# The head of a pooling and state-space layer: x scaled before it is transposed, dt taken from unsplit h, and another written order

## Chip, cores, metric

The kernel runs on one core of a Trainium2 chip. The metric is the time of one execution in microseconds (us) as the device measures it; lower is better. Times are medians of several runs on the same chip.

A core has five engines with an instruction stream each: TensorE (PE in the profile, its weight loads PEld), VectorE (DVE), ScalarE (ACT), GpSimd (POOL) and SyncE (SP), which here only issues DMA transfers. ACT issues some DMAs too. Results of matmuls go to PSUM, everything else on the chip to SBUF.

## The reference, cut to what matters

One layer of inference on a prompt of 1024 rows and 64 sample rows (8 sequences of 8), 1088 rows of 1024 channels together, all in fp32:

```
shift, scale, gate = split(silu(c) @ w_ada + b_ada, 3)
h = rmsnorm(x, norm_g) * (1 + scale) + shift
u_pool, z_pool, z_ssm, xbc, dt_raw, g_raw = split(h @ w_in)
p  = (pool_mix(u_pool) * silu(z_pool)) @ w_pool_out
dt = softplus(dt_raw + dt_bias)
y  = ssd(silu(conv(xbc)), dt, ...) ; y = rmsnorm(y * silu(z_ssm), ssm_norm_g)
s  = y @ w_ssm_out
x  = x + gate * ((sigmoid(g_pool) * p + sigmoid(g_ssm) * s) @ w_o)
out = rmsnorm(x, final_g)
```

Outputs are the normalised rows and the new states of the pooling, the convolution and the recurrence.

## The kernel before, in words

Matmuls of full precision are made from reduced-precision ones: an operand is split into a high part (`whi`, `hh_`) made by ACT and a low part (`wlo`, `hl_`), the rest, made by DVE or POOL; a product is then three matmuls, high by high, high by low and low by high. h is kept transposed, channels on partitions: eight tiles `tf[k]` of 128 channels by 1088 rows in fp32, and `hh_[k]`, `hl_[k]`.

The change lies in `first()`, the head, and in what it calls. There the order on all five engines is the written one: `in_line` chains the instructions of each engine as they are written. Behind it a scheduler orders by priority, and may put instructions of later units between those of `first()`.

The head runs through these stages:

1. **Turning x.** Nine row tiles (eight of 128 rows, one of 64) are loaded. For each, the sum of squares is taken by DVE or ACT (`x_square`), then a root by ACT (`x_root`) and a reciprocal by DVE (`x_unit`), in groups of rows 0 and 1, 2 to 4, 5 to 8. `x_unit` also builds for each row tile the diagonal matrix of the reciprocals, and `x_turn` multiplies x by it on PE (L228), which transposes and scales at once. `x_copy` takes the result from PSUM to `tf`, by DVE and ACT in turn. A step is one group and one k; `x_turns(2, ...)` is the third group, block 2 of the columns. PSUM comes in 5 buffers `ps` (`PB()`) and 3 buffers `mm` (`PA()`).
2. **Coefficients.** `ada_mm`, `ada_out`, `ada_end` compute scale and shift (`md`) in three parts, for k 0 and 1, 2 and 3, and 4 to 7. `ada_end` transposes the result (L286).
3. **h.** `h_make(block, ks)` applies scale and shift: ACT writes the high part, DVE or ACT the fp32 value in place in `tf`, DVE the low part (L309).
4. **First products.** `products(block, ks)` makes two tiles of the sigmoid gate from h and weights directly (L883 to L885). `done` applies the sigmoid and stores. `gate_load` and `gate_mm` (L839) make the residual gate in eight steps on the side; four loads wait until an earlier step frees a buffer.
5. **dt.** `dt_block` multiplies h by 32 columns of `w_in` (L733), in four column groups of PE. It reads high and low part one after the other, both as fp32.
6. **Sums.** `combine()` makes the sums of blocks of h that a Strassen-Winograd scheme with seven products needs (S1, S2, S3, and S4, which replaces parts of `hh_` and `hl_`), in the place of `tf`, and splits them: high halves by ACT (L481, L504), low halves by DVE (L482, L497). It is a generator; each `next(sums)` issues a piece.
7. **First pair.** `strassen(..., early=True)` runs the seven products of a pair of output tiles; a product is 24 matmuls with 272 columns (L603 to L605). Its weights w[0] to w[6] are prepared by `first_steps` (differences L549, splits L160 and L163, low parts by DVE), stepped by `next(wst)`. `hook(n)`, called behind product n, issues the sums and weight splits that later products need. Products 3 (the fourth), 4, 5 and 6 read S2, S3, S1 and S4.

After the head come the other pairs, in the same scheme with POOL making the low parts, then the pooling and state-space work.

Of the kernel before, what the change touches and what calls it, by code (L numbers as in the profile page):

```python
# [8 lines left out]
F32 = mybir.dt.float32  # L9
F32R = mybir.dt.float32r  # L10
AF = mybir.ActivationFunctionType
ALU = mybir.AluOpType
# [8 lines left out]
P = 128  # L21
# [20 lines left out]
HF, SB = T // 2, T // 4  # L42
# [4 lines left out]
def tile_pool_ssd_step(  # L47
# [9 lines left out]
    def nm(s):  # L57
        uid[0] += 1
        return f"{s}_{uid[0]}"
# [30 lines left out]
    def R(shape=(P, T), dt=F32):  # L90
        return hs.tile(list(shape), dt, tag="R", name=nm("R"), bufs=3)
# [7 lines left out]
    def PA():  # L99
        return psA.tile([P, 512], F32, tag="mm", name=nm("mm"))  # L100
# [108 lines left out]
    def x_unit(a, b):  # L209
        n = xr[a][1]  # L210
        V.reciprocal(rs[:n, a:b], rs[:n, a:b])
        if not dg:
            dg.append(R())
        for i in range(a, b):
            n = xr[i][1]
            V.tensor_scalar(dg[0][:n, i * P:i * P + n], ident[:n, :n], rs[:n, i:i + 1], None, ALU.mult)

    tf = [None] * KT

    def x_turn(g3, k):  # L220

        if g3 == 0:
            tf[k] = tfp.tile([P, T], F32, tag="tf", name=nm("tf"), bufs=8)
        px = PB()
        c = 0
        for i in range((0, *XG)[g3], XG[g3]):
            xt, n = xr[i]
            mm(px[:, c:c + n], xt[:n, k * P:(k + 1) * P], dg[0][:n, i * P:i * P + n], start=True, stop=True)  # L228
            c += n
        return g3, k, px, c  # L230

# [243 lines left out]
    def combine():  # L475
        L_, R_ = slice(0, HF), slice(HF, T)

        big = []

        def parts(src, hi, lo):  # L480
            act(hi, src, AF.Copy)  # L481
            V.tensor_tensor(lo, src, hi.bitcast(F32), ALU.subtract)  # L482

        def room(lst, k):
            if lst is S1:
                lst[k] = (hs.tile([P, 2, HF], F32R, tag="sq", name="S1", bufs=1) if k == 3 else R((P, 2, HF), F32R))
            else:
                if k == 0:
                    big.append(Y4(hs).rearrange("p k (j n) -> p k j n", j=2))
                lst[k] = big[-1][:, k]  # L490

        def part(lst, k, src):
            room(lst, k)
            parts(src, lst[k][:, 0], lst[k][:, 1])

        def low(k):
            V.tensor_tensor(S2[k][:, 1], tf[k][:, L_], S2[k][:, 0].bitcast(F32), ALU.subtract)  # L497
        for k in range(4):
            a, b = tf[k], tf[k + 4]
            room(S2, k)  # L500
            V.tensor_tensor(b[:, R_], a[:, R_], b[:, R_], ALU.add)
            V.tensor_tensor(a[:, R_], a[:, L_], a[:, R_], ALU.subtract)
            V.tensor_tensor(a[:, L_], b[:, R_], a[:, L_], ALU.subtract)
            act(S2[k][:, 0], a[:, L_], AF.Copy)  # L504
            if k:
                low(k - 1)
            if k < 3:
                yield
        low(3)
        yield  # L510
        for k in range(4):
            part(S3, k, tf[k][:, R_])
        yield
        for k in range(4):
            a, b = tf[k], tf[k + 4]
            V.tensor_tensor(b[:, L_], b[:, L_], a[:, L_], ALU.subtract)
            part(S1, k, b[:, R_])
            if k % 2:
                yield
        for k in range(4):  # L520
            parts(tf[k + 4][:, L_], hh_[k][:, R_], hl_[k][:, R_])
            if k % 2:
                yield

# [196 lines left out]
    def dt_w():  # L721
        raw = tfp.tile([P, KT, NH], F32, tag="dtw", name="dtw", bufs=1)
        load(raw, w_in[0, :, C_DT:C_DT + NH].rearrange("(k p) c -> p k c", p=P))
        return raw

    def dt_block(w, i):
        o, n = BLK[i]
        ps = PA()
        for kk in range(2):
            for part in (hh_, hl_):  # L730
                for r in range(4):
                    k = 4 * kk + r
                    mm(ps[32 * r:32 * r + 32, :n], w[:, k, :], part[k][:, o:o + n].bitcast(F32),  # L733
                       start=(kk == 0 and part is hh_), stop=(kk == 1 and part is hl_))
        s = pa.tile([P, HF], F32, tag=("s1", "u2", "u3")[i], name=nm("dts"))
        act(s[:, :n], ps[:, :n], AF.Identity, bias=dtb[:, 0:1])
        store_(dts_d[:, o:o + n], s[:, :n])

# [115 lines left out]
    def first():  # L854
# [14 lines left out]

        banks = {}  # L870

        def products(bi, ks):
            o, n = BLK[bi]
            for t in range(2):
                if (bi, t) not in banks:
                    banks[bi, t] = (PB if (bi, t) in ((1, 1), (2, 0), (2, 1)) else PA)()[:, :n]
            for k in ks:
                for t in range(2):
# [4 lines left out]
                    mm(ps, a, rh, start=(k == 0), stop=False)  # L883
# [3 lines left out]
        tags = iter(("s1", "u2", "u3", "c2", "s1", "u2"))  # L887

        def done(bi, t):
            o, n = BLK[bi]  # L890
# [66 lines left out]
        for k in range(4, 8):  # L957
            ada_load(2, k)
        next(late)
        mr = ada_out(1)  # L960
        products(2, range(1))
        ada_end(1, mr)
# [11 lines left out]
        for k in range(4, KT):  # L974
            ada_mm(2, k)
        mr = ada_out(2)
        products(2, range(3, 4))
        dtw = dt_w()
        run, (wz, wst) = light[0][1], light[0][0]()
        bg = gate_bias()  # L980
        for k in range(4):
            gate_load(k)
        next(wst)
        ada_end(2, mr)

        for bi in range(3):
            h_make(bi, range(4, 8))
        for bi in range(3):
            products(bi, range(4, 8))
            for k in range(2 * bi, min(2 * bi + 2, 4)):  # L990
                gate_mm(k)
                gate_load(k + 4)

        sums = combine()
        next(late)
        for bi in range(3):
            done(bi, 0)
            done(bi, 1)
            next(sums)
        dt_block(dtw, 0)  # L1000
        dt_block(dtw, 1)
        next(sums)
        next(wst)
        dt_block(dtw, 2)
        next(sums)
        for k in range(4, 8):
            gate_mm(k)
        gate_end(bg)
        next(late, None)

        def hook(n):
            if n in (0, 2):
                next(wst)
            if n < 2:
                next(sums)
            if n in (3, 4):
                next(wst)
                next(sums)
        run(wz, hook)
        in_line(every)  # L1020
# [915 lines left out]
```

## Time and profile before

| | |
|---|---|
| Median of 3 runs | 1301.33 us (1299.25 to 1301.85) |
| Profiled execution: its own time | 1298.25 us |
| Profiled execution: span | 1296.5 us, 26406 instructions |
| PE busy | 1261.6 us |
| DVE, ACT, POOL busy | 887.8, 696.2, 675.4 us |
| Granted clock of PE, mean | 0.996 |
| HBM | 167.06 MB read, 83.01 MB written |

In the time-order rows a line gives start, length, engine, line of the kernel, operation, result and operands, shapes and count, and in brackets the idle time of the engine just before and what ended it. Rows of groups give busy us and mean ns of one, then idle time. An fp32 matmul leaves two records, a transpose one. Ends of matmuls are modelled, since they are pipelined; starts are the better measure on PE.

### The profile page before, as it was taken

To read this page: it belongs to the slowest core of one execution; us is meant where nothing else is said; L and a number is where in the kernel's file an instruction comes from. 1 tells how busy PE (TensorE), PEld (TensorE's weight loads), DVE (VectorE), ACT (ScalarE), POOL (GpSimd) and SP (SyncE) were. 2 spreads that over 40 slices of the span, in tenths; PEclk is the share of its full clock that TensorE was granted. 3 is DMA by queue.
4 is the path that set the end of the run, shared out by engine and by line. 5 is a ranking of instruction groups with operands and counts; after the bars stand their busy time and mean duration, and the time that the engine had idled before them with its cause. 6 is when DMAs were issued, how large, how long until landed. Compare 5 with 4: busy or idle time off the path is not lost. (4 is left out here: it accounts for less than half of the span.)

```text
span 1296.5 us, 26406 instructions
## 1 busy us (share of the span) xinstructions
PE 1261.6 (97%) x9739; PEld 1168.5 (90%) x9739; DVE 887.8 (68%) x1512; ACT 696.2 (54%) x1656; POOL 675.4 (52%) x563
## 2 busy tenths in 40 slices
PE   7999999999999999999999999999999999999998
PEld 6779999989999999998889999888888888999786
DVE  4685778866978678775767665477565878476433
ACT  5664356375656564545455464676887766201111
POOL 1007668677869776664344453366676656214000
PEclk9999999999999999999999999999999999999999
DMA  9837345465455544444556455999988665475631
GB/s 331 255 110 232 109 157 174 136 212 162 153 183 198 157 159 129 159 135 128 160 154 194 148 170 174 346 358 364 312 282 277 203 204 163 170 268 160 228 105 50
DMA packets 233793, 251.68 MB, mean 194 GB/s; under 512 B 31265, under 2 KB 177905, under 8 KB 233658
## 3 DMA queue, kind: packets, MB, share of 16 engines
q1 hardware_dynamic: 161568, 171.60, 41.7%
q10 hardware_dynamic: 72098, 78.41, 17.6%
q8 instruction: 77, 1.26, 0.4%
q14 instruction: 50, 0.41, 0.1%
HBM read 167.06 MB, written 83.01 MB: 193 GB/s over the span
## 5 line engine op out<-in xcount | busy, mean ns | idle before, releaser
L163 POOL TENSOR_TENSOR wlo<-rawA,whi 128x512 fp32r<-128x512 f32 x120 | 185.3, 1549 | 188.1 <-ACT whi L160 101.7
L163 POOL TENSOR_TENSOR wlo<-raw,whi 128x512 fp32r<-128x512 f32 x92 | 151.1, 1650 | 121.9 <-ACT whi L160 112.8
L354 PE MATMUL mm<-Y,whi 128*128 128x352 f32 (+1 forms) x480 | 163.3, 340 | 0.9 <-DVE G L1785 0.7
L355 PE MATMUL mm<-Y,whi 128*128 128x352 f32 (+1 forms) x480 | 157.4, 328 | 1.0 <-DVE Y L1459 1.0
L356 PE MATMUL mm<-Y,wlo 128*128 128x352 f32 (+1 forms) x480 | 156.8, 327 | 0.0
L605 PE MATMUL mm<-Y,wlo 128*128 128x272 f32 x496 | 143.6, 290 | 4.5 <-POOL wlo L163 4.1
L603 PE MATMUL mm<-Y,whi 128*128 128x272 f32 x496 | 146.4, 295 | 0.2
L603 PE MATMUL ps<-Y,whi 128*128 128x272 f32 x496 | 144.4, 291 | 1.4 <-ACT o L803 1.4
L604 PE MATMUL ps<-Y,whi 128*128 128x272 f32 x496 | 143.1, 289 | 0.0
L604 PE MATMUL mm<-Y,whi 128*128 128x272 f32 x496 | 142.9, 288 | 0.0
L605 PE MATMUL ps<-Y,wlo 128*128 128x272 f32 x496 | 142.6, 288 | 0.0
L160 ACT ACTIVATE whi<-rawA 128x512 fp32r<-128x512 f32 x125 | 78.1, 626 | 97.0 <-PE ps L604 43.2
L1051 DVE SCALAR_TENSOR_TENSOR GA<-GA,cvT,GA 128x1112 f32<-128x1112 f32 x72 | 126.7, 1763 | 0.6 <-ACT GA L1048 0.5
L160 ACT ACTIVATE whi<-raw 128x512 fp32r<-128x512 f32 x96 | 58.7, 626 | 91.2 <-DVE raw L549 43.0
L605 PEld LDWEIGHTS mm<-Y,wlo 128*128 128x128 f32 x496 | 93.4, 188 | 6.4 <-POOL wlo L163 5.4
L354 PEld LDWEIGHTS mm<-Y,whi 128*128 128x128 f32 x480 | 90.2, 188 | 6.9 <-issue 4.3
L603 PEld LDWEIGHTS ps<-Y,whi 128*128 128x128 f32 x496 | 93.3, 188 | 2.7 <-ACT o L803 1.6
L603 PEld LDWEIGHTS mm<-Y,whi 128*128 128x128 f32 x496 | 93.3, 188 | 2.3 <-issue 0.8
L604 PEld LDWEIGHTS mm<-Y,whi 128*128 128x128 f32 x496 | 93.4, 188 | 0.7 <-issue 0.6
L604 PEld LDWEIGHTS ps<-Y,whi 128*128 128x128 f32 x496 | 93.3, 188 | 0.3 <-issue 0.2
L605 PEld LDWEIGHTS ps<-Y,wlo 128*128 128x128 f32 x496 | 93.4, 188 | 0.2 <-issue 0.2
L1196 ACT ACTIVATE dec<-dec,acT 128x128 f32<-128x128 f32 (+1 forms) x288 | 86.7, 383 | 10.0 <-POOL dec L1187 6.3
(445 smaller groups left out, 3790.3 us busy)
## 6 DMA issues: line engine op xcount, KB each, us to landing
rawA<-in_w_in SPq DMA_DIRECT2D x46, 512.0 KB
dec<-acs_d SPq DMA_DIRECT2D x32, 512.0 KB
xbc<-GA ACTq DMA_DIRECT2D x24, 512.0 KB
xb<-xbc SPq DMA_DIRECT2D x32, 384.0 KB
rawA<-in_w_in SPq DMA_DIRECT2D x32, 256.0 KB
pw<-in_w_ssm_out ACTq DMA_DIRECT2D x32, 256.0 KB
ws<-ph ACTq DMA_DIRECT2D x32, 256.0 KB
ws<-pw SPq DMA_DIRECT2D x32, 256.0 KB
```

The source lines that it names most:

```text
L160: ins = act(hi[:, :, :ncols], raw[:, :, :ncols], AF.Copy)
L163: (eng or nc.gpsimd).tensor_tensor(lo[:, :, :ncols], raw[:, :, :ncols], hi[:, :, :ncols].bitcast(F32), ALU.subtract)
L354: mm(ps[:, :n], a, rh[k][:, o:o + n], start=(k == 0), stop=False)
L355: mm(ps[:, :n], a, rl[k][:, o:o + n], start=False, stop=False)
L356: mm(ps[:, :n], b, rh[k][:, o:o + n], start=False, stop=(k == nk - 1))
L603: mm(p, hi, ah, start=(k == 0), stop=False)
L604: mm(p, hi, al, start=False, stop=False)
L605: mm(p, lo, ah, start=False, stop=(k == 3))
L1051: V.scalar_tensor_tensor(d[:, :n], rp[:, k:k + n], cvT[:, 24 * k + mc:24 * k + mc + 1], d[:, :n], ALU.mult, ALU.add)
L1196: act(dec[:, h], dec[:, h], AF.Exp, bias=acT[:S, c, 8 * g + h:8 * g + h + 1], scale=-1.0)
```

## The change

- Rows 0 and 1 of x are turned as before. Rows 2 to 8 are scaled in place by their reciprocals (3, 6 and 8 by ACT, the others by DVE), and turned by a transpose against the identity.
- `dt_block` reads h from `tf` before the sums overwrite it, with half the matmuls; its bias, copy and store become `dt_out`. Blocks 0 and 1 come behind `products(1, ...)`, block 2 in front of the last product step of block 2. Then come the sums.
- The sums come in another order: the second and third weight step are put in front of and behind S2; S3 behind product 0, S1 in one piece behind product 2 without the last subtraction; this stands directly in front of each S4 split, behind products 3 and 4.
- The products of block 2 with k = 3 are halved around the third `ada_end`; h and products of blocks 0, 1, 2 alternate; the sigmoids of block 0 come before the h of block 2.
- `dt_w` and some buffer tags are moved.

```diff
         if not dg:
-            dg.append(R())
+            dg.append(R((P, 2 * P)))
         for i in range(a, b):
-            n = xr[i][1]
-            V.tensor_scalar(dg[0][:n, i * P:i * P + n], ident[:n, :n], rs[:n, i:i + 1], None, ALU.mult)
+            xt, n = xr[i]
+            if i < 2:
+                V.tensor_scalar(dg[0][:n, i * P:i * P + n], ident[:n, :n], rs[:n, i:i + 1], None, ALU.mult)
+            elif i in (3, 6, 8):
+                act(xt[:n], xt[:n], AF.Copy, scale=rs[:n, i:i + 1])
+            else:
+                V.tensor_scalar(xt[:n], xt[:n], rs[:n, i:i + 1], None, ALU.mult)
...
-            mm(px[:, c:c + n], xt[:n, k * P:(k + 1) * P], dg[0][:n, i * P:i * P + n], start=True, stop=True)
+            if i < 2:
+                mm(px[:, c:c + n], xt[:n, k * P:(k + 1) * P], dg[0][:n, i * P:i * P + n], start=True, stop=True)
+            else:
+                nc.tensor.transpose(px[:, c:c + n], xt[:n, k * P:(k + 1) * P], ident[:n, :n])
...
         for k in range(4):
+            part(S1, k, tf[k + 4][:, R_])
+        yield
+        for k in range(4):
             a, b = tf[k], tf[k + 4]
             V.tensor_tensor(b[:, L_], b[:, L_], a[:, L_], ALU.subtract)
-            part(S1, k, b[:, R_])
-            if k % 2:
-                yield
-        for k in range(4):
-            parts(tf[k + 4][:, L_], hh_[k][:, R_], hl_[k][:, R_])
+            parts(b[:, L_], hh_[k][:, R_], hl_[k][:, R_])
             if k % 2:
                 yield
...
-        ps = PA()
+        ps = (PA if i < 2 else PB)()
         for kk in range(2):
-            for part in (hh_, hl_):
-                for r in range(4):
-                    k = 4 * kk + r
-                    mm(ps[32 * r:32 * r + 32, :n], w[:, k, :], part[k][:, o:o + n].bitcast(F32),
-                       start=(kk == 0 and part is hh_), stop=(kk == 1 and part is hl_))
-        s = pa.tile([P, HF], F32, tag=("s1", "u2", "u3")[i], name=nm("dts"))
+            for r in range(4):
+                k = 4 * kk + r
+                mm(ps[32 * r:32 * r + 32, :n], w[:, k, :], tf[k][:, o:o + n], start=(kk == 0), stop=(kk == 1))
+        return ps
+
+    def dt_out(i, ps):
+        o, n = BLK[i]
+        s = pa.tile([P, HF], F32, tag=("u3", "c2", "s1")[i], name=nm("dts"))
         act(s[:, :n], ps[:, :n], AF.Identity, bias=dtb[:, 0:1])
         store_(dts_d[:, o:o + n], s[:, :n])
...
         mr = ada_out(2)
-        products(2, range(3, 4))
-        dtw = dt_w()
+        products(2, range(3, 4), (0,))
...
+        ada_end(2, mr)
+        products(2, range(3, 4), (1,))
+        h_make(0, range(4, 8))
+        products(0, range(4, 8))
+        gate_mm(0)
+        gate_load(4)
+        h_make(1, range(4, 8))
         next(wst)
-        ada_end(2, mr)
-        for bi in range(3):
-            h_make(bi, range(4, 8))
-        for bi in range(3):
-            products(bi, range(4, 8))
-            for k in range(2 * bi, min(2 * bi + 2, 4)):
-                gate_mm(k)
-                gate_load(k + 4)
+        products(1, range(4, 8))
+        done(0, 0)
+        done(0, 1)
+        dts = [dt_block(dtw, i) for i in range(2)]
+        h_make(2, range(4, 8))
+        products(2, range(4, 7))
+        dts.append(dt_block(dtw, 2))
+        for i in range(3):
+            dt_out(i, dts[i])
+        products(2, range(7, 8))
+        for k in range(1, 4):
+            gate_mm(k)
+            gate_load(k + 4)
+        next(late)
+        next(wst)
         sums = combine()
-        next(late)
-        for bi in range(3):
-            done(bi, 0)
-            done(bi, 1)
-            next(sums)
-        dt_block(dtw, 0)
-        dt_block(dtw, 1)
+        next(sums)
+        done(1, 0)
+        done(1, 1)
+        next(sums)
+        next(sums)
+        done(2, 0)
+        done(2, 1)
         next(sums)
         next(wst)
-        dt_block(dtw, 2)
-        next(sums)
         for k in range(4, 8):
             gate_mm(k)
         gate_end(bg)
         next(late, None)
         def hook(n):
-            if n in (0, 2):
+            if n in (1, 3, 4):
                 next(wst)
-            if n < 2:
-                next(sums)
-            if n in (3, 4):
-                next(wst)
+            if n in (0, 2, 3, 4):
                 next(sums)
```

More of the change, by code (lines that the diff above doesn't have):

```diff
@@ L870, in first, with products @@
         banks = {}
-        def products(bi, ks):
+        def products(bi, ks, ts=range(2)):
             o, n = BLK[bi]
@@ L877, in products @@
             for k in ks:
-                for t in range(2):
+                for t in ts:
                     ps = banks[bi, t]
@@ L885, in products @@
                     mm(ps, a, rl, start=False, stop=(k == KT - 1))
-        tags = iter(("s1", "u2", "u3", "c2", "s1", "u2"))
+        tags = iter(("s1", "u2", "u2", "u3", "c2", "s1"))
         def done(bi, t):
@@ L959, in first @@
         next(late)
+        dtw = dt_w()
         mr = ada_out(1)
```

## Prediction

> **What bounds the kernel now.** I read the page first, then the chain of waits of TensorE, then the head of the kernel in time order, engine by engine, since every edit lies in the first 105 us.
>
> ```profile
> span 1296.5 us, 26406 instructions
> PE 1261.6 (97%) x9739; PEld 1168.5 (90%) x9739; DVE 887.8 (68%) x1512; ACT 696.2 (54%) x1656; POOL 675.4 (52%) x563
> ```
>
> TensorE (PE) is busy 97% of the span and idle 35 us in all. Whoever wants time must take work from PE, or the place where PE waits; and work taken from PE counts only where PE is what ends last. So I cut the head into stretches (columns: length, then busy us of PE, PEld, VectorE = DVE, ScalarE = ACT, GpSimd = POOL with instruction counts, granted clock, DMA share, GB/s).
>
> ```profile
> 9.70:10.70 1.00, 1.00 (x4) 1.00 (x5) 1.00 (x2) 0.46 (x2) 0.00 (x0) 1.00 1.07 418
> 11.70:12.70 1.00, 1.00 (x7) 1.00 (x6) 0.04 (x1) 0.90 (x2) 0.00 (x0) 1.00 0.99 397
> 13.70:14.70 1.00, 1.00 (x11) 1.00 (x11) 0.91 (x5) 0.41 (x2) 0.00 (x0) 1.00 0.88 165
> 66.40:79.30 12.90, 12.90 (x147) 7.17 (x146) 11.42 (x18) 8.04 (x16) 0.00 (x0) 1.00 0.52 190
> 79.30:100.00 20.70, 20.12 (x157) 19.67 (x157) 19.04 (x34) 13.71 (x26) 1.76 (x1) 1.00 0.24 75
> ```
>
> Two things show. From 66.4 to 100 us DVE is busy 30.5 of 33.6 us: it is nearly as full as PE, with the sums of h. And PE's first matmuls run slowly: 4, then 7, then 11 records in a microsecond of the same work, although the granted clock says 1.00 throughout.
>
> **Turning x.** Now the rows that price the first edit.
>
> ```profile
> 20.39 0.94 PE L228 MATMUL ps<-R,Y 128*128 128x128 f32 x6
> 21.25 0.43 PE L228 MATMUL ps<-R,R 64*128 64x64 f32 x2
> 21.61 0.94 PE L228 MATMUL ps<-R,Y 128*128 128x128 f32 x6
> ...
> 29.77 0.33 PE L286 MATMUL ps<-ident,mr 128*128 128x128 f32 x1
> ...
> 50.91 0.47 PE L883 MATMUL ps<-Y,whi 128*128 128x448 f32 x1
> 52.23 0.38 PE L286 MATMUL ps<-ident,mr 128*128 128x128 f32 x2
> ...
> 834.38 0.60 PE L1400 MATMUL ps<-ident,xb 128*128 128x128 f32 x4
> 834.81 0.27 PE L1402 MATMUL ps<-ident,xb 128*128 128x128 f32 x1
> ```
>
> Each matmul of x by a diagonal leaves two records. A step of the third group (rows 5 to 8) takes 21.61 - 20.39 = 1.22 us, three full rows of it 0.86. A transpose against the identity leaves one record, and four take 834.81 - 834.38 = 0.43, so 0.11 each: a third-group step becomes 0.44, a second-group step (rows 2 to 4) 0.32 instead of 0.86. On PE that removes 8 x 0.78 + 8 x 0.54 = 10.6 us. The other end is the cadence of L228's records, 0.86 / 6 = 0.14, which would leave 1.0 to 1.5 us of it behind; I take 0.11, from the same instruction.
>
> The price is on the other engines: seven rows of 1024 must be scaled before they can be turned.
>
> ```profile
> 13.97 0.68 DVE L216 TENSOR_SCALAR R<-ident,rs 128x128 f32<-128x128 f32 x3
> 17.43 1.22 DVE L201 SCALAR_TENSOR_TENSOR sqj<-Y 128x1024 f32<-128x1024 f32 x1
> ...
> 19.42 0.29 ACT L207 ACTIVATE rs<-ss,eps 128x4 f32<-128x4 f32 x1
> 19.74 0.18 DVE L211 RECIPROCAL rs<-rs 128x4 f32<-128x4 f32 x1 [0.62 <-ACT rs L207]
> ...
> L1896 DVE TENSOR_SCALAR q<-q,sso 128x640 f32<-128x640 f32 x1 | 0.6, 553 | 0.1
> L203 ACT ACTIVATE sqj<-Y 128x1024 f32<-128x1024 f32 x3 | 3.1, 1046 | 0.0
> ```
>
> A diagonal costs DVE 0.68 / 3 = 0.23; a row scaled by DVE lies between the 0.55 of 640 elements and the 1.22 of the two-read operation on 1024. Between 0.23 at 128 and 0.55 at 640 lies 0.63 ns an element, so 1024 take an estimated 0.79. ACT takes 1.05 for 1024. At the second group DVE scales two rows instead of building three diagonals (+0.9), which moves its last square from 17.43 to about 18.3 and its end to 19.5: about when the root of the last four stood ready anyway (19.42). The four rows behind the reciprocal then need two scalings on DVE and, longer, two on ACT: 19.9 + 2 x 1.0 = 21.9. So the third group starts at 21.9 instead of 20.39, later by 1.5, with PE out of work from about 18.7 (the second group can start behind its last scaled row, 13.97 + 2 x 0.75 = 15.5, works 2.6 and waits a little for its copies out of PSUM).
>
> From there to L286 (29.77), where the first coefficients are turned, lie six steps of 1.22 and 2.06 us of the coefficients' own matmuls. After: 21.9 + 5 x 0.44 + 2.06, plus some 0.45 for the copy out of PSUM, which the sixth step covers now: 26.6. The 10.6 us of PE work have become 3.2 us. Everything up to the last product of this stage is a chain through those coefficients, ACT, DVE and PE in turn, and moves by the same 3.2; the third coefficients wait for half a product step instead of a whole one (50.91 to 52.23), which adds 0.7.
>
> The quiet stretch costs again. In before's rows PE needed three microseconds at about half rate after its quiet start. A quiet 3.2 us ahead of the third group is likely to bring that back: half rate for 3 us loses 1.5. I take it. The Trainium skill (TensorE: Matmul & The Clock Gate, part 1) says the same of an idle window of about 3.4 us; part 4 of that page adds that transposes do not count as activity for the clock, which speaks against this change, since then the whole group runs at half rate. No row of before shows turns by transposes right after a quiet stretch, so that is kept as a rival below.
>
> **dt from unsplit h.**
>
> ```profile
> 69.73 1.07 PE L733 MATMUL mm<-Y,dtw 128*32 128x256 f32 x16
> 77.06 1.48 PE L839 MATMUL ps<-R,scT 128*32 128x256 f32 x24
> ```
>
> The three dt blocks take 77.06 - 69.73 = 7.33 us; one operand instead of two halves that: -3.67 on PE. But they now stand in front of the sums, because the sums overwrite h.
>
> ```profile
> 66.40 0.70 DVE L501 TENSOR_TENSOR tf<-tf,tf 128x544 f32<-128x544 f32 x1
> ...
> 78.20 0.72 DVE L497 TENSOR_TENSOR Y<-tf,Y 128x544 fp32r<-128x544 f32 x1 [1.21 <-ACT Y L504]
> 78.84 1.28 DVE L163 TENSOR_TENSOR wlo<-rawA,whi 128x512 fp32r<-128x512 f32 x2
> 80.16 0.69 DVE L549 TENSOR_TENSOR rawA<-raw,rawA 128x512 f32<-128x512 f32 x1
> 80.84 2.63 DVE L482 TENSOR_TENSOR Y<-tf,Y 128x544 fp32r<-128x544 f32 x4
> ...
> 85.20 0.71 DVE L516 TENSOR_TENSOR tf<-tf,tf 128x544 f32<-128x544 f32 x1
> 87.74 0.43 DVE L619 TENSOR_TENSOR c<-s,mm 128x272 f32<-128x272 f32 x1
> 90.08 0.72 DVE L482 TENSOR_TENSOR R<-tf,R 128x544 fp32r<-128x544 f32 x1 [0.93 <-ACT R L481]
> 97.85 2.46 DVE L482 TENSOR_TENSOR Y<-tf,Y 128x544 fp32r<-128x544 f32 x2
> ...
> 78.07 1.14 ACT L160 ACTIVATE whi<-rawA 128x512 fp32r<-128x512 f32 x2
> 79.11 0.62 ACT L736 ACTIVATE dts<-mm,dtb 128x448 f32<-128x448 f32 x1
> 80.14 2.31 ACT L481 ACTIVATE Y<-tf 128x544 fp32r<-128x544 f32 x4 [0.41 <-ACT dts L736]
> 88.20 0.78 ACT L715 ACTIVATE c<-c 128x272 f32<-128x272 f32 x2 [1.71 <-DVE c L619]
> 89.39 0.66 ACT L481 ACTIVATE R<-tf 128x544 fp32r<-128x544 f32 x1 [0.40 <-ACT c L715]
> 98.58 0.28 PE L603 MATMUL mm<-Y,whi 128*128 128x272 f32 x1
> 104.48 0.29 PE L605 MATMUL ps<-Y,wlo 128*128 128x272 f32 x1
> ```
>
> Before, DVE began the sums at 66.40, 3.3 us before the products were done and 10.7 before dt was. After, call T the end of the last dt block. Products end at 69.73 now; less 3.9 of the head, less the last step of the products (1.3) and three gate steps (1.48) which now come behind dt, plus 3.67 of halved dt: T = 66.7 with a fast clock, 68.2 with the slow stretch. On ACT dt's copy and its store (80.14 - 79.11 = 1.0) stand ahead of the next weight split, which takes 0.6 (L160), so DVE resumes at T + 1.7. Then in written order on DVE:
>
> - weight splits and a difference (78.84 to 80.84): 2.0, T + 3.7
> - the first sums and their low parts (66.40 to 78.84, less the 1.21 waited): 11.2, T + 14.9
> - two splits (1.3), gate and bias copies (0.6), S3's low parts (2.6): T + 19.4
> - two adds of 0.35 behind a product; then a split that waits about 1.6 for ACT (two activations and a store, 88.20 to 89.39, then the high half): T + 22.3
> - S1's low parts with a first wait of 0.5: T + 25.4; two adds, a difference, a split waiting 0.6: T + 28
> - the last four parts, where each subtraction is now directly followed by its own high and low half. Before they were apart, and only ACT waits show; now DVE 0.64, ACT 0.6, DVE 0.64 and two hand-overs stand in line, 2.05 for each: 8.2 in place of the 5.2 that four L516 and four L482 take. With two adds and a split (1.3): T + 37.5.
>
> PE without any wait would need from T only the product step (1.3), seven gate steps and transposes (3.9) and six products of 3.0 (98.58 to 104.6 holds two): T + 23 for the first operand of the seventh. So DVE's chain sets the end: the seventh product has its last operand at T + 37.5 and is done 2.0 later, T + 39.5. That is 106.2 with a fast clock, 107.7 with the slow stretch. In before the seventh product and one product of the next pair are done at 104.6. In after that one has room in PE's gaps (some 16 us). So PE comes out of the head later by 1.6 or 3.1 us, and behind it PE is the bound again, with the same work.
>
> The gate rows' loads now follow their release at once: three of 512 KB at 418 GB/s need an estimated 3.8 us, in which PE waits. That costs nothing while the third product waits for its weights from DVE (T + 16.1); without that cover it costs up to 3.8.
>
> **The sum** against the profiled execution (1298.25 us on the clock of the runs, 1296.5 span, 1.75 around it): -3.9 head, +1.5 clock, +5.5 for DVE's chain, which starts later and is longer: +3.1 in all, 1301.4. The profiled execution lies 3.1 below the median of 1301.33, so I give the forecast on the median: 1304.4.
>
> **Rivals.**
> 1. The clock stays fast through the third group: +1.6, 1302.9. For it: the quiet stretch is 3.2 us only, with transposes shortly before.
> 2. The transposes do not wake PE at all: all eight steps at 0.88, 3.5 lost instead of 1.5: +5.1, 1306.4. In the rows only the slow start speaks for it. By part 4 of the Trainium skill's page TensorE: Matmul & The Clock Gate this would be the likelier of the two.
> 3. The gaps are used: not one but three products of the next pair, 3.0 each, move into the 16 us in which PE waits: 1.6 - 6.0 = -4.4, 1296.9. It decides if the next pair's weights, whose load needs a buffer that DVE's split at T + 28 frees, arrive some 5 us ahead of T + 37.5. Against it: those splits need the same DVE. For it: outside this stage the order of instructions is free.
> 4. PE stays the bound all through, and the whole 10.6 + 3.67 of removed work shows: 1287. Against it stands DVE's 30.5 of 33.6 us.
> 5. No gap is filled at all: +6.1 with the slow stretch, 1307.4.
>
> **Chances.** Forecast and near it (over 0.2% slower) 0.28, rival 2 0.10, rival 5 0.07; rival 1 and its neighbourhood within 0.2%, 0.25; rival 3 0.23, rival 4 0.07. A measurement of this kernel can tell about 0.2% (2.6 us) from no change. So slower 0.45, same 0.25, faster 0.30. The range leaves out rival 4 and a tail: 1295.5 to 1309, from 1.4 below rival 3 to 1.6 above rival 5; that margin is the unknown price of a scaled row (0.55 to 1.22, in the two scalings on the path).
>
> **What would show it.** Right: third-group transposes starting at 21 to 22 us with PE idle some 3 us before; few records per microsecond there; first sums near T + 3.7; waits of PE for DVE in the fifth to seventh product; the seventh product's end near 107. Wrong: sums early, or products of the next pair standing between those of this one, so that PE has no gaps from 85 to 105.

## The result and the profile after

After takes 1311.03 us (median; 1308.30 to 1315.05), before on the same chip 1299.25 us (1298.04 to 1301.85): ratio 1.0087, 95% interval 1.0061 to 1.0113. That is 11.8 us more, where 3.1 were forecast, and outside the forecast's range of 1295.5 to 1309.0; the direction was the forecast's.

The page of after, span and first line of part 1:

```profile
span 1306.5 us, 26198 instructions
PE 1261.2 (97%) x9635; PEld 1165.1 (89%) x9635; DVE 888.4 (68%) x1509; ACT 698.2 (53%) x1659; POOL 676.2 (52%) x563
```

PE is as busy as before (1261.2 to 1261.6 us) although 104 matmul records are gone. The stretches of the head show why (columns as in the prediction: length, busy us of PE, PEld, DVE, ACT, POOL, granted clock, DMA share, GB/s). After:

```profile
20.39:29.77 9.38, 8.61 (x84) 5.80 (x84) 3.44 (x8) 4.12 (x7) 2.75 (x3) 0.64 1.10 352
66.40:79.30 12.90, 9.57 (x85) 5.20 (x83) 7.37 (x13) 4.98 (x10) 0.00 (x0) 0.93 0.49 174
79.30:100.00 20.70, 19.61 (x141) 18.02 (x138) 17.72 (x31) 12.90 (x25) 0.00 (x0) 0.88 0.15 54
100.00:110.00 10.00, 5.54 (x33) 5.13 (x32) 7.36 (x11) 2.95 (x5) 1.26 (x1) 0.74 0.22 63
110.00:120.00 10.00, 8.30 (x46) 7.88 (x46) 6.04 (x11) 5.71 (x13) 6.13 (x5) 0.75 0.46 147
```

Before, the first of these and the two that the prediction does not show:

```profile
20.39:29.77 9.38, 9.38 (x114) 7.86 (x113) 3.02 (x9) 2.81 (x6) 2.74 (x3) 1.00 1.10 347
100.00:110.00 10.00, 9.45 (x73) 9.01 (x73) 6.16 (x12) 6.07 (x14) 7.74 (x6) 1.00 0.63 211
110.00:120.00 10.00, 10.00 (x82) 10.00 (x82) 5.93 (x13) 3.94 (x9) 7.04 (x6) 1.00 0.71 209
```

Before, the clock is 1.00 in all of them. After, it is 0.64 to 0.93, and PE is idle besides. A busy PE at half clock does about half the work (48 matmuls that take 1.52 us at full clock take 2.79 at half, below): that is why its busy time did not fall.

The loss can be placed by one row. The first product of the pooling work stands behind the whole head; from the third pair on, the instructions of all kernels here stand in the same order on every engine, but for single neighbours. The two numbers after "ns" are its first and last start. Before, then after:

```profile
L809 PE MATMUL ps<-GA,pwt x24: 379/486/539, 166.5 to 473.3; 128*128 128x256 f32 x8, 128*128 128x384 f32 x8, 128*128 128x448 f32 x8
```
```profile
L818 PE MATMUL ps<-GA,pwt x24: 379/486/540, 179.7 to 484.1; 128*128 128x256 f32 x8, 128*128 128x384 f32 x8, 128*128 128x448 f32 x8
```

It starts 13.2 us later (179.7 - 166.5), and the span ends 10.0 later. So the head holds the loss, and the start of this row is the marker for the experiments. Summing windows of 1 us from 9 us to the marker splits that time in three: PE idle, PE's loss to the clock (busy time times one minus granted clock), and the work at full clock that is left. (Neither trace has a clock record ahead of 12.6 us; the views count the clock there as 1.00, so the 1.00 that the prediction read beside the slow first matmuls says nothing of them.)

| kernel | marker | idle | clock loss | work |
|---|---|---|---|---|
| before | 166.5 | 4.5 | 0.0 | 153.0 |
| after | 179.7 | 16.2 | 10.3 | 144.2 |

The change does remove 8.8 us of PE work; it adds 11.7 us of idle time and 10.3 of slow clock.

**The head in time order.** PE after:

```profile
14.79 3.72 PE L236 MATMUL ps<-ident,Y 128*128 128x128 f32 x24
20.73 0.90 PE L236 MATMUL ps<-ident,Y 128*128 128x128 f32 x3 [2.02 <-DVE Y L221]
22.07 0.27 PE L236 MATMUL ps<-ident,R 64*128 64x64 f32 x1 [0.44 <-ACT R L219]
...
22.96 0.90 PE L236 MATMUL ps<-ident,Y 128*128 128x128 f32 x3
23.79 0.37 PE L236 MATMUL ps<-ident,R 64*128 64x64 f32 x1
24.09 0.90 PE L236 MATMUL ps<-ident,Y 128*128 128x128 f32 x3
...
25.22 2.79 PE L279 MATMUL ps<-Y,scT 128*32 128x128 f32 x48
...
30.60 0.33 PE L294 MATMUL ps<-ident,mr 128*128 128x128 f32 x1
...
69.29 1.71 PE L739 MATMUL ps<-tf,dtw 128*32 128x448 f32 x16
...
77.05 0.71 PE L848 MATMUL ps<-R,scT 128*32 128x256 f32 x8 [2.78 <-DMA R<-in_w_ada]
78.31 1.08 PE L848 MATMUL ps<-R,scT 128*32 128x256 f32 x8 [0.56 <-DMA R<-in_w_ada]
...
107.34 0.56 PE L610 MATMUL mm<-Y,whi 128*128 128x272 f32 x1 [3.57 <-DVE s L621]
...
113.05 0.39 PE L610 MATMUL mm<-Y,whi 128*128 128x272 f32 x1 [1.17 <-ACT Y L489]
```

A step of the third group takes 24.09 - 22.96 = 1.13 us, hardly less than the 1.22 of before; the first coefficients are turned at 30.60, later than before's 29.77. The last dt block ends at 71.00 (69.29 + 1.71): this is T. DVE after, from there:

```profile
74.84 0.72 DVE L509 TENSOR_TENSOR tf<-tf,tf 128x544 f32<-128x544 f32 x1
...
84.72 1.53 DVE L505 TENSOR_TENSOR Y<-tf,Y 128x544 fp32r<-128x544 f32 x2
...
87.98 2.62 DVE L490 TENSOR_TENSOR Y<-tf,Y 128x544 fp32r<-128x544 f32 x4
...
95.87 0.72 DVE L490 TENSOR_TENSOR S<-tf,S 128x544 fp32r<-128x544 f32 x1
...
98.58 0.69 DVE L163 TENSOR_TENSOR wlo<-rawA,whi 128x512 fp32r<-128x512 f32 x1 [0.69 <-ACT whi L160]
...
103.25 0.69 DVE L556 TENSOR_TENSOR raw<-rawA,rawA 128x512 f32<-128x512 f32 x1 [1.26 <-DMA rawA<-in_w_in]
103.97 1.64 DVE L556 TENSOR_TENSOR raw<-raw,rawA 128x512 f32<-128x512 f32 x1
105.53 0.68 DVE L556 TENSOR_TENSOR rawA<-rawA 128x512 f32<-128x512 f32 x1
...
113.03 0.88 DVE L490 TENSOR_TENSOR Y<-tf,Y 128x544 fp32r<-128x544 f32 x1 [2.17 <-ACT Y L489]
```

The rows at 103.25 to 105.53 are weight differences of the next pair: the scheduler put them between the S4 parts of this one, the first of them waiting 1.26 us for a load. ACT has the same in front of the last S4 part, two weight splits of the next pair:

```profile
111.30 0.63 ACT L160 ACTIVATE whi<-rawA 128x512 fp32r<-128x512 f32 x1 [1.83 <-DMA rawA<-in_w_in]
```

The 2.17 us for which DVE waits at 113.03 come from there. Of the next pair's products, half a one (12 matmuls from 107.34 on) stands ahead of the end of the seventh product.

### The profile page after: what moved, and what is told of

The parts are those of the page before. It is cut to its first block, busy times and chain, and to the rows that moved or that the text cites. A ratio compares the mean times of both kernels' runs of the same rounds, so it can differ in the third digit from the quotient of the medians.

```text
span 1306.5 us, 26198 instructions
## 1 busy us (share of the span) xinstructions
PE 1261.2 (97%) x9635; PEld 1165.1 (89%) x9635; DVE 888.4 (68%) x1509; ACT 698.2 (53%) x1659; POOL 676.2 (52%) x563
## 4 chain that ended last, share of the span: by engine, by line
PE 33%; issue 6%; POOL 4%; DMA 4%; DVE 2%; ACT 2%; SPq 0%; ACTq 0%; POOLq 0%; DVEq 0%
PE mm L362 3%; PE mm L363 2%; PE mm L364 2%; PE ps L1900 2%; PE ps L1901 2%; PE ps L1902 2%; PE ps L610 2%; PE ps L612 2%; PE ps L611 2%; PE mm L612 2%; PE mm L610 2%; PE mm L611 2%; PE ps L1226 2%; PE ps L1442 1%; PE ps L1307 1%
## 5 line engine op out<-in xcount | busy, mean ns | idle before, releaser
L610 PE MATMUL mm<-Y,whi 128*128 128x272 f32 x496 | 148.3, 299 | 6.0 <-DVE s L621 3.6
L611 PE MATMUL mm<-Y,whi 128*128 128x272 f32 x496 | 144.8, 292 | 0.5 <-DVE Y L490 0.5
L160 ACT ACTIVATE whi<-rawA 128x512 fp32r<-128x512 f32 x125 | 77.9, 626 | 92.5 <-PE ps L611 42.3
L610 PEld LDWEIGHTS mm<-Y,whi 128*128 128x128 f32 x496 | 94.9, 191 | 8.5 <-issue 4.3
L611 PEld LDWEIGHTS mm<-Y,whi 128*128 128x128 f32 x496 | 95.0, 192 | 1.4 <-DVE Y L490 0.7
L362 PEld LDWEIGHTS mm<-Y,whi 128*128 128x128 f32 x480 | 90.3, 188 | 6.6 <-issue 4.3
L363 PEld LDWEIGHTS mm<-Y,whi 128*128 128x128 f32 x480 | 90.4, 188 | 1.7 <-DVE Y L1477 1.6
```

The costliest lines, as they stand in the source:

```text
L160: ins = act(hi[:, :, :ncols], raw[:, :, :ncols], AF.Copy)
L362: mm(ps[:, :n], a, rh[k][:, o:o + n], start=(k == 0), stop=False)
L363: mm(ps[:, :n], a, rl[k][:, o:o + n], start=False, stop=False)
L610: mm(p, hi, ah, start=(k == 0), stop=False)
L611: mm(p, hi, al, start=False, stop=False)
```

## Experiments

Each ratio is to before on the same chip; the marker is the start of the first pooling product in the profiled execution.

**Each half alone.** "x only" is before with the new `x_unit` and `x_turn`, as below against before; "order only" is after with these lines turned back:

```diff
+            elif i in (3, 6, 8):
+                act(xt[:n], xt[:n], AF.Copy, scale=rs[:n, i:i + 1])
+            else:
+                V.tensor_scalar(xt[:n], xt[:n], rs[:n, i:i + 1], None, ALU.mult)
...
+                nc.tensor.transpose(px[:, c:c + n], xt[:n, k * P:(k + 1) * P], ident[:n, :n])
```

> The kernel before with the turning of x alone (seven rows scaled and transposed), everything else in the old order. Theory: the gain of the transposes is eaten by TensorE's half clock, so the first coefficients are turned at 30.6 us as in the changed kernel (29.8 before), and the third at about 52.5; the time is that of before within 1.5 us (a ratio of 0.999 to 1.001). Rival A (turning x is the loss): the ratio is 1.005 or more. Rival B (turning x is a real gain that the new order throws away): 0.997 or less.

> The changed kernel with x turned by diagonal matrices as before: the new place of dt and the new order alone. Theory: nearly the whole loss is here, +9 to +13 us (1.007 to 1.010): sums from about 74 us instead of 66.4, the gate's last loads waited for, the seventh product done near 118 instead of about 104.5. Rival A (turning x is the loss): less than +5 us.

x only: 1306.46 us, ratio 1.0057 (1.0034 to 1.0081), marker 168.2. Order only: 1312.59 us, 1.0097 (1.0065 to 1.0129), marker 177.8. At the marker +1.7 and +11.3 add to 13.0, against 13.2: the halves hardly disturb each other. By its time x only is where rival A put it (1.005 or more), by its marker it is not: the time was more than the marker explains, which is taken up below.

**What in x costs.** The filled kernel is x only with eight idle matmuls while PE waits for the scaled rows:

```diff
         v_turn()
+        pd = PB()
+        for _ in range(8):
+            mm(pd[:, :P], ident, ident, start=True, stop=True)
         x_turns(2, range(4))
```

> x turned as in the changed kernel, everything else in the old order, and 8 idle matmuls of 128 columns on the identity in the quiet 2 us of TensorE ahead of the third group of rows; they add work and no result. Theory A (the quiet stretch halves the clock): the clock stays at 1.00 from 22 to 30 us, the first coefficients are turned near 27 us instead of 30.6, the first pooling product comes at 163 to 165 (168.2 without the filling, 166.5 before), and the time is 0 to 4 us below that of before. Theory B (transposes do not count as activity): the clock is halved all the same, about as long, and nothing is gained: first coefficients at 30 or later, 168 to 169.

1299.40 us, ratio 0.9983 (0.9966 to 0.9999), marker 165.4. PE of this kernel, time order:

```profile
19.01 2.05 PE L941 MATMUL ps<-ident 128*128 128x128 f32 x16
20.90 0.91 PE L236 MATMUL ps<-ident,Y 128*128 128x128 f32 x3
...
22.45 0.55 PE L236 MATMUL ps<-ident,Y 128*128 128x128 f32 x3
22.92 0.27 PE L236 MATMUL ps<-ident,R 64*128 64x64 f32 x1
23.13 0.55 PE L236 MATMUL ps<-ident,Y 128*128 128x128 f32 x3
...
24.48 1.52 PE L279 MATMUL ps<-Y,scT 128*32 128x128 f32 x48
...
27.87 0.33 PE L294 MATMUL ps<-ident,mr 128*128 128x128 f32 x1
```

Its row of the stretch from 18 to 31 us:

```profile
18.00:31.00 13.00, 11.98 (x128) 8.78 (x128) 7.79 (x20) 8.99 (x18) 2.76 (x3) 1.00 1.10 348
```

The clock stays at 1.00 throughout, a step takes 0.68, the coefficients' 48 matmuls 1.52 instead of 2.79, and the first coefficients come at 27.87. So the quiet 2 us ahead of the group cost 2.7 us (30.61 in x only to 27.87) through the clock that followed. The head's clock stayed at 1.00 in all six profiled executions with idle matmuls in this gap, here and below, and fell in all seven that turn x in the new way without them.

**What in the order costs.** "dt only" is before with the unsplit, halved dt in front of the sums, and nothing else but the new places of the first sigmoids and two buffer tags that follow from it:

```diff
-        sums = combine()
         next(late)
+        done(0, 0); done(0, 1)
+        dts = [dt_block(dtw, i) for i in range(3)]
+        for i in range(3):
+            dt_out(i, dts[i])
+        sums = combine()
...
-        dt_block(dtw, 0)
-        dt_block(dtw, 1)
```

> The kernel before with dt from unsplit h directly in front of the sums, behind all products; x, sums and hooks in the old order (only the places of the first sigmoids and two buffer tags follow). Theory (what costs is that the sums, VectorE's chain, start behind dt): the sums start near 74 instead of 66.4 and the first pooling product comes 5 to 9 us later than before (171 to 175), although TensorE has 3.7 us less to do. Rival (the new order of sums and weight splits is the loss, dt costs nothing): no later than 1 us (up to 167.5).

1308.89 us, ratio 1.0058 (1.0038 to 1.0078), marker 174.7: 8.2 us of the 11.3. Its first sum on DVE, and its first Strassen product on PE:

```profile
73.76 0.73 DVE L501 TENSOR_TENSOR tf<-tf,tf 128x544 f32<-128x544 f32 x1 [7.14 <-PE ps L732]
```
```profile
85.00 0.59 PE L603 MATMUL mm<-Y,whi 128*128 128x272 f32 x1 [9.11 <-ACT whi L160]
```

DVE has done all of h and stands for 7.14 us, waiting for dt; the sums start 7.4 us later than before's 66.40, and PE pays 9.11 us for it at the next stage, while dt itself, 69.88 to 73.75, takes 3.9 us instead of 7.3. Up to the marker 8.8 us of idle time and 3.2 of slow clock are added, and 3.8 of work are saved.

"Subtraction early" (sub early) is after with the last subtraction back in S1's loop:

```diff
         for k in range(4):
+            a, b = tf[k], tf[k + 4]
+            V.tensor_tensor(b[:, L_], b[:, L_], a[:, L_], ALU.subtract)
             part(S1, k, tf[k + 4][:, R_])
         yield
         for k in range(4):
-            a, b = tf[k], tf[k + 4]
-            V.tensor_tensor(b[:, L_], b[:, L_], a[:, L_], ALU.subtract)
-            parts(b[:, L_], hh_[k][:, R_], hl_[k][:, R_])
+            parts(tf[k + 4][:, L_], hh_[k][:, R_], hl_[k][:, R_])
```

> The changed kernel with the last subtraction put back in front of the low halves of S1, so that the last four parts need no subtraction of their own. Theory: VectorE's chain loses four hand-overs of 0.7 us, and the next pair's differences no longer stand inside it, so the seventh product is done 5 to 8 us earlier than in the changed kernel and the time is +3 to +6 us over before (1.002 to 1.005). Rival (the chain is long anyway, because it starts late): no more than 2 us better than the changed kernel, +8 to +10.

1309.63 us, ratio 1.0072 (1.0049 to 1.0095), marker 175.5: 4.2 us earlier than after; that is less than was expected (5 to 8) and more than the rival allowed (2), while the time, 9.4 us above before, lies in the rival's range (8 to 10). If the parts add up, x (1.7), dt (8.2) and this (4.2) make 14.1 of 13.2 us, and what else the change reorders gains about 1.

"Held" is after with the next pair's weight steps set behind all else on DVE and ACT, as long as the head runs:

```diff
             prep_q.remove(prep)
+            if held:
+                held.pop()
+                with behind(mybir.EngineType.DVE), behind(mybir.EngineType.Activation):
+                    for _ in prep:
+                        pass
```

> The changed kernel with the next pair's differences and splits of weights issued behind the head's last instructions of VectorE and ScalarE, so that they cannot stand inside the last parts of the sums; the order of the head itself is unchanged. Theory: the last low half comes 4 us earlier (near 110 instead of 113.9), but the next pair's second product comes later by a part of that: +6 to +9 us over before (1.005 to 1.007). Rival (the intrusion only used idle time): no better than the changed kernel, or worse, +10 to +13.

1314.76 us, ratio 1.0117 (1.0080 to 1.0154), marker 179.5, as after. The last S4 low part did end earlier (111.06 against 113.91), but then the next pair's differences ran from 115.04 on, and PE waited 1.00 us for their split at 118.17. The intrusion moves the wait and does not make it: both are work of the same DVE in front of the same products. The theory that it was the loss falls.

"Gate back" is after with the first four residual-gate steps between the first products, where before had them:

```diff
-        gate_mm(0)
-        gate_load(4)
+        for k in range(2):
+            gate_mm(k)
+            gate_load(k + 4)
...
         products(1, range(4, 8))
+        for k in range(2, 4):
+            gate_mm(k)
+            gate_load(k + 4)
...
-        for k in range(1, 4):
-            gate_mm(k)
-            gate_load(k + 4)
```

> The changed kernel with the gate steps 1 to 3 and the loads behind them put back between the products of h, where they were. Where it stands is read at the first pooling product (166.5 us before, 179.7 in the changed kernel). Theory (VectorE's chain sets the end of the head): TensorE's 3.3 us of waiting for the gate rows and the half clock behind it go, but the first pooling product comes at most 2 us earlier (177.5 to 180). Rival (the wait and the clock it costs are the loss): 4 to 7 us earlier (173 to 176), and a time of +4 to +7 over before.

1318.44 us, ratio 1.0142 (1.0118 to 1.0166), marker 180.1. The 3.3 us of waiting for gate rows are gone and the clock loss falls from 10.3 to 5.5 us, but the idle time grows from 16.2 to 19.6: PE came to its next wait for DVE and ACT sooner. Neither that wait nor the slow clock beside it bounds this stretch in after. The time is 7 us above after's all the same; that lies behind the marker and is taken up below.

"dt in front" is after with the third dt block and the three copies ahead of the last four product steps:

```diff
-        products(2, range(4, 7))
         dts.append(dt_block(dtw, 2))
         for i in range(3):
             dt_out(i, dts[i])
-        products(2, range(7, 8))
+        products(2, range(4, 8))
```

> The changed kernel with the last dt block in front of all product steps of block 2 instead of behind three of them. Theory (VectorE's chain, which starts with the last dt block, sets the end): the sums start 3 us earlier (71 to 72 instead of 74.8) although TensorE waits about 1 us for h, and the first pooling product comes 2 to 4 us earlier (176 to 178). Rival (TensorE's own waits and clock set the end): no earlier, or later by the 1 us waited (179 to 181).

1315.66 us, ratio 1.0120 (1.0090 to 1.0149), marker 178.2. dt ended at 66.6, 4.4 us earlier (about 1 of it because the head's slow stretch lasted 3.4 us in this execution, 23.7 to 27.1, and the first coefficients came at 29.63), but DVE began the sums only 3.0 earlier:

```profile
69.94 1.29 DVE L163 TENSOR_TENSOR wlo<-rawA,whi 128x512 fp32r<-128x512 f32 x2 [2.98 <-ACT whi L160]
71.27 0.69 DVE L556 TENSOR_TENSOR rawA<-raw,rawA 128x512 f32<-128x512 f32 x1
71.88 0.72 DVE L509 TENSOR_TENSOR tf<-tf,tf 128x544 f32<-128x544 f32 x1
```

The weight splits written ahead of the sums hold them up: they wait for ACT, which has dt's three copies and stores first. And half of the 3.0 us was lost again before the marker.

**Mended.** "After filled" is after with the eight idle matmuls. "Mended" is that with the subtraction early, dt in front, and the weight splits behind the second part of the sums; "mended with gate" has the gate steps back as well:

```diff
         next(late)
-        next(wst)
         sums = combine()
         next(sums)
         done(1, 0)
         done(1, 1)
         next(sums)
+        next(wst)
         next(sums)
```

> After, with eight idle matmuls ahead of the third group of x, nothing else. Theory that the slow clock of the head is passed on through the coefficients, h, dt and the sums one after the other: coefficients, sums and first pooling product all some 2.5 us earlier than after's 30.6, 74.84 and 179.7, so 28, 72.3 and 177. Rival: the sums or a load set the end whatever the head does: 179.7 as after.

> After with four pieces put right together: eight idle matmuls ahead of the third group, the last dt block in front of the last four product steps, the weight splits behind the first sums, the subtraction back with S1. Theory that VectorE's chain from the sums to the last low part sets the end, by its start and its length: sums start at 64.5 to 65.5 as in the kernel before, although dt now stands in front of them, and the first pooling product at 165 to 168, against 166.5 before and 179.7 after; time 0.997 to 1.001 of before. Rival: the loads of the gate rows, no longer under cover, take the place: 3 to 4 us more, 169 to 171.

> The kernel before this one, with the first four steps of the residual gate between the first products, where the kernel before had them. Theory of VectorE's chain: as the mended kernel within 1 us, 165 to 168, since TensorE has room there. Rival of the gate rows' loads: 3 to 4 us earlier than the mended kernel, because the second four loads are in flight 10 us earlier.

| kernel | first sum | marker | idle | clock loss | work | time | ratio |
|---|---|---|---|---|---|---|---|
| after filled | 72.64 | 178.6 | 15.6 | 7.7 | 146.3 | 1308.80 | 1.0059 (1.0036 to 1.0082) |
| mended | 66.07 | 170.2 | 10.4 | 5.1 | 145.8 | 1301.09 | 1.0004 (0.9985 to 1.0024) |
| mended with gate | 65.74 | 168.0 | 10.2 | 2.7 | 146.1 | 1298.83 | 0.9996 (0.9975 to 1.0018) |

The sums started nearly where they were expected, and 9.5 of the 13.2 us came back; with the gate steps 11.7. Mended missed its range by 2.2 us, and the rival was right about those: with the chain shorter, the 3 us wait for gate rows counts; the gate steps took 2.2 us off, between the two expectations (under 1, and 3 to 4). The longest wait of PE that is left behind the start of the last kernel is this one:

```profile
94.35 0.59 PE L610 MATMUL mm<-R,whi 128*128 128x272 f32 x1 [4.02 <-ACT whi L160]
```

From 93.0 to 99.8 us the clock is halved once more. Filling after alone gave 2.2 us at the coefficients and the sums, but 1.1 at the marker; the rest is lost again on the way.

**Behind the head.** Two kernels were measured again, and two with a pure delay were added: nineteen idle matmuls instead of eight in the filled kernel, and eleven in before.

> The kernel before with x turned as after and eight idle matmuls ahead of the third group (the kernel x filled once more, in five rounds). If what the first half of the change wins is only the clock kept at 1.00 and 2.4 us of earlier first coefficients, the first pooling product starts 1 us earlier than before's 166.5, so about 165.4, and the time lies 1 to 2 us below before, ratio 0.998 to 0.9995. Rival: the 1.7 us of the first measurement was chance, and five rounds give 1.000 with an interval that holds it.

> The kernel before with x turned as after and nothing else, once more in five rounds. The head alone explains 1.7 us (first pooling product at 168.2 against 166.5), but the time was 7 us longer. Theory that the rest came from stretches at half granted clock behind the head that fall by chance: ratio 1.001 to 1.004 this time, and those stretches at other places. Rival that a head that comes 2.7 us later with a slow stretch leaves the later stages in a worse rhythm: 1.0057 again, with a half-clock stretch near 265 us again.

> The filled kernel with nineteen idle matmuls instead of eight: TensorE stays busy and at clock 1.00, and the first coefficients come 2.7 us later, at 30.6, as in the kernel with x alone. Theory that a delay of the head is passed on one to one and no more: 2.8 us above the filled kernel, first pooling product at 168.2, ratio 1.000 to 1.002. Rival of the rhythm: as x alone, 1.0057.

> The kernel before with eleven idle matmuls ahead of the third group of x: the head is 2.8 us later, nothing else. Theory one to one: first pooling product at 169.3, ratio 1.0022. Rival of the rhythm: 1.005 or more.

| kernel | marker | time | ratio |
|---|---|---|---|
| filled, again | 165.7 | 1297.83 | 0.9984 (0.9966 to 1.0001) |
| x only, again | 168.3 | 1303.02 | 1.0022 (1.0005 to 1.0040) |
| filled, 2.3 us later | 167.7 | 1300.33 | 0.9990 (0.9976 to 1.0005) |
| before, 3.5 us later | 170.0 | 1304.55 | 1.0033 (1.0011 to 1.0055) |

A delay at full clock costs no more than itself, within the intervals: 3.5 us at the marker of before make 4.3 in the time (0.0033 of 1300.26), 2.3 in the filled kernel 0.8 (0.0006). x only came out at 1.0022, 2.9 us for the 1.8 of its marker, with the same order and the same head; its slow stretch at 265 us was gone, and the mean granted clock of its runs was 0.991 instead of 0.989. Behind the marker its two profiled executions take 1135.6 and 1131.4 us: of these 4.2 us, 1.6 are slow clock and 2.5 idle PE. So the first measurement's excess lay behind the head and does not come each time, and the theory of a lasting rhythm has nothing left to explain. What starts these late losses stays open.

The same holds of gate back and dt in front, whose times lie 7 and 5 us above after's at markers of +0.4 and -1.5. From the marker to the end they take 1136.4 and 1132.4 us, after 1126.8 and before 1130.0, with the same order of work; PE is idle there for 26.9, 25.0, 21.1 and 22.4 us. The markers, not these times, carry the argument about the head.

The filled kernel stands 0.17% and 0.16% below before in its two measurements, and the second interval reaches 1.0001: at the edge of what can be told. No kernel here beats before clearly.

## Why the prediction was wrong, step by step

| step | predicted | measured in after |
|---|---|---|
| third group starts | 21.9 | 20.73, its row 8 at 22.07 |
| a step at full clock | 0.44 | 0.68 (filled kernel) |
| first coefficients | 28.1 | 30.60 |
| T, last dt block done | 68.2 | 71.00 |
| first sum | T + 3.7 | T + 3.8 |
| S2, S3, S1 low parts done | T + 14.9, 19.4, 25.4 | T + 15.2, 19.6, 25.6 |
| split behind S1 done | T + 28 | T + 28.3 |
| last S4 low part done | T + 37.5 | T + 42.9 |

**Right:** that DVE's chain behind dt, not PE, sets the end of the head; the chain's terms up to T + 28, within 0.3 us each; dt's halving; that the gate rows' loads cost nothing while DVE is later (the gate steps back gained nothing). Rivals 3 and 4 fall: of the next pair only half a product stands in the gaps, where the forecast had one and rival 3 three. Rival 5, with none, is the nearest in mechanism, and it too is too small.

**Wrong, first step: the slow clock ("half rate for 3 us loses 1.5").** The slow stretch lasted 6.8 us (0.64 granted over the 9.38 us from 20.39), ran through the coefficients' matmuls too, and cost 2.7 us at the first coefficients. I had taken its length from before's quiet start. The length is not the same each time: in five of the seven executions with this gap it was 6.8 us, in gate back and dt in front 3.4, with the first coefficients at 29.29 and 29.63.

**Wrong, second step: the price of a transpose.** I chose 0.11, start to start, over 0.14. Groups of before and of the filled kernel settle it (busy us, mean ns):

```profile
L228 PE MATMUL ps<-R,Y 128*128 128x128 f32 x128 | 18.0, 296 | 2.0 <-DVE R L216 2.0
```
```profile
L236 PE MATMUL ps<-ident,Y 128*128 128x128 f32 x48 | 8.1, 286 | 0.1
```

48 transposes fill 8.1 us, 0.17 each; the end of the range that I left was too low as well. Why the four at 834.38 were quicker stays open. PE work removed by x is 6.2 us (146.8 left in x only, 153.0 before) and not 10.6. These two steps make most of the 2.8 us by which T is late (2.5 at the first coefficients); rival 2's price of 3.5 us was nearer, but not its reason (below).

**Wrong, third step: the last S4 parts (T + 37.5).** They ended 5.4 us later, with the next pair's differences and the wait for their load between them. I had priced only instructions of the written order, although I had noted that the scheduler may put others between. Holding those back did not help: the right term is all the work that DVE and ACT have in front of the next products, the next pair's included.

The two delays, 2.8 and 5.4 us, added to the forecast's 3.1 give 11.3, against 13.2 at the marker. That sum is arithmetic and not shown: filling after moved the sums by 2.2 us and the marker by 1.1. The half product for which the gaps had no room would be 1.5 more, by the prediction's 3.0 for a whole one. **Not priced at all** was what a gap does to the clock after it: the forecast had some 16 us of gaps behind T and let PE leave them at full speed. Three more slow stretches, 77.5 to 84.3, 104.8 to 111.6 and 115.0 to 118.4, bring the clock loss to 10.3 us. It does not simply add: beside a stretch that waits for DVE anyway it costs nothing, as the gate kernel showed.

On the clock, the Trainium skill (TensorE: Matmul & The Clock Gate, part 4) says that the full clock does not engage for transposes, which do not count as busy in the same way. In the filled kernel PE ran nothing but transposes from 20.90 to 24.48 (0.44 us of it waiting) and kept 1.00. Since the clock changes in steps of 3.4 us (last section), that stretch might owe its clock to the matmuls at its two ends; but in mended with gate a whole step, 21.28 to 24.70, has transposes alone but for its last 0.04 us, and the clock is 1.00 in it and in the next one (columns as in the prediction):

```profile
21.28:24.70 3.42, 2.98 (x22) 1.84 (x23) 2.30 (x6) 2.00 (x4) 0.00 (x0) 1.00 1.10 346
24.70:28.11 3.41, 3.41 (x74) 2.54 (x74) 0.63 (x2) 1.86 (x4) 2.20 (x2) 1.00 1.10 351
```

So transposes by themselves did not cost the clock; the quiet ahead of them did. Whether they are slower than other matmuls in bringing it back stays open: in x only, again, a step filled with transposes alone (22.49 to 25.90) was followed by another at half clock, but the slow stretch at 77.5 in after, with two small ones in it, was as long.

## What to carry to other kernels

Halving an operation's work can cost more than it saves if it must now stand between two stages of the engine that is nearly full: price the move by when that engine's next chain starts (here 8.4 us), not by the work saved (3.5). Price a gap on PE by the gap and by the slow stretch that follows it, and, if the gap cannot go, try whether a few idle matmuls inside it keep the clock. Where a scheduler may mix in later work, count all that stands on the engine in front of the next consumer, not the written order alone.

## What the hardware showed that I had not expected

- The clock changes on a grid of 3.41 us. From after's first fall at 22.88 to the next ones (77.49, 104.80, 115.04) it is 16, 24 and 27 times 3.413. Slow stretches are whole steps long: 3.4 us (115.0 to 118.4 in after), 6.8 us (the head's, 77.5 to 84.3, 104.8 to 111.6), and 13.7 us in dt only (77.9 to 91.5). In another execution the grid lies elsewhere: the fall in the head came at 22.88 in after, at 21.25 in sub early. The Trainium skill (TensorE: Matmul & The Clock Gate, part 1) gives a free-running window of about 3.4 us, and the trace agrees.
- In the head 2.0 us without any work, and 0.4 more, were enough, and the clock fell only at 22.9, two microseconds after PE had resumed. The Trainium skill (TensorE: Matmul & The Clock Gate, part 1) has as a rule no idle gaps above about 3.4 us; this gap was shorter and cost the clock. Nor does the busy time of a step decide alone: one with 2.04 us of it was followed by a fall (51.18 to 54.59 in the filled kernel), one with 1.64 was not (72.45 to 75.86 in sub early).
- Eight idle matmuls of the identity (2.05 us) in such a gap kept the clock at 1.00.
- Between runs of one kernel a longer time goes with a lower mean granted clock: over the twelve runs of the filled kernel's second measurement, 0.993 to 0.998, about 1 us for each 0.001 (correlation 0.76). This is a good part of the scatter that hides differences of 2 us here.
